# The first 256 tokens' output projection, memory attention and feed-forward as a thread of the attention stage

## The chip, the cores and the metric

The kernel runs on one core of a Trainium2 chip. The metric is the device time of one execution in microseconds (us), as the median of several executions. PE is TensorE (PEld its weight loads), DVE is VectorE, ACT is ScalarE, POOL is GpSimd, SP is SyncE, which here only issues transfers (SPq is its queue).

## The reference, cut to what matters

One layer of a hybrid decoder for 1024 prompt tokens and 8 sample tokens, width 1024, in float32:

```python
h = rmsnorm(x, attn_norm_g)
q, k, v, qi, ki, wi, gq, gk, gv, gz, ga, gb = split(h @ w_in)
o_attn = sparse_attend(q, k, v, top 256 keys by the indexer)     # 8 heads of 64, causal
o_gdn  = gated_delta_chunked(conv(gq, gk, gv), ga, gb)           # 4 heads of 128, recurrent over tokens
x = x + concat([o_attn, o_gdn]) @ w_out                          # 1024 x 1024
x = x + mem_attend(rmsnorm(x), mem_k, mem_v, w_mq, w_mo)         # 4 heads, 256 memory tokens
hf = rmsnorm(x)
x = x + (silu(hf @ w_gate) * (hf @ w_up)) @ w_down               # D_FF = 2816
```

Attention and recurrence are causal: a token's row depends on earlier tokens only, and everything from `w_out` on works on each token alone.

## The kernel before, in words

Each projection is done in three products of rounded parts: a weight arrives by one transfer as `raw`, ACT rounds it to `wh` (L124), POOL subtracts to get `wl` (L125), and for each of eight slices of the contraction PE multiplies `wh` by the high and by the low part of the activations and `wl` by the high part (`proj`, L128 to L139). So one weight of 1024 x 128 costs 24 matmuls for a group of tokens. Activations stand transposed, 128 features on the partitions and tokens along the row, in `AH` and `AL`.

Three stages follow each other in `build` (L1811).

1. **Front**: norm of x, input projections, indexer scores, the top-k searches on DVE, and the preparation of the recurrence (`gdn_prep`, and `gdn_invert` for heads 0 and 1).
2. **Attention stage** (L1853 to L1871): `run` (L69) steps six generators in turn, each at a rate: `stage_attend` (query tiles 7 down to 0, four head pairs each), two threads `gdn_scan` (heads 0, 2 and heads 1, 3, each head through its four quarters of 256 tokens), the sample tokens' gather and attention, their recurrence, and `gdn_invert(1)`, a row by row inversion on POOL that the merges of heads 2 and 3 need. The logits use the PSUM banks `al` (two), transposes use `at` (two).
3. **Tail** (`stage_mem`, `stage_ffn`): all 1032 tokens in the groups `GROUPS2` of 512, 256 and 264. `stage_out` multiplies by `w_out`, `mem_q` and `mem_attend` are the memory attention, `mem_out` multiplies by `w_mo`, and the feed-forward goes in batches of four of its 22 blocks of 128 (`gate_up`, then `down`). `stage_mem_kv` (L1506), which makes the keys and values of the memory, runs beside the first `stage_out`.

The generators only set the program order and a priority number (`cur_priority`, L78). At build time the tile framework replays the program against a model of the engines and from that fixes one order for each engine; on the chip each engine works through its list in that order and waits where an operand is late. Every buffer is a slot of a pool with a fixed number of slots, and transfers that SP issues wait in SP's list for their slot.

```python
self.run([self.stage_attend(qs), 1, 0], [self.scan_pair("a", 0, 2), 0.3, 0], [self.scan_pair("b", 1, 3), 0.3, 0],
         [chain(self.stage_sample_rows(), self.stage_sample_attend()), 0.25, 300],
         [chain(*(self.gdn_sample(h) for h in range(4))), 0.2, 0], [self.gdn_invert(1), 1.0, 300])
```

Of the kernel before, what the change touches and what calls it, by code (L numbers as in the profile page):

```python
# [6 lines left out]
F32 = mybir.dt.float32  # L7
# [13 lines left out]
NS = 8  # L21
# [3 lines left out]
GROUPS2 = ((0, 512), (512, 256), (768, 264))  # L25
# [12 lines left out]

class Kernel:
    def __init__(self, tc, ins, outs):  # L40
        self.tc, self.nc, self.i, self.o = tc, tc.nc, ins, outs
        self.side, self.G = [], GROUPS
        self.set, self.set_users = None, []
# [40 lines left out]

    def drain(self):
# [31 lines left out]
    def raw_w(self, kt, n):  # L117
        return self.wp.tile([128, kt, n], F32, name="raw", tag="raw", bufs=2)

    def split_w(self, raw):  # L120
        shape = list(raw.shape)
        wh = self.wp.tile(shape, FR, name="wh", tag="wh", bufs=2)
        wl = self.wp.tile(shape, FR, name="wl", tag="wl", bufs=2)
# [206 lines left out]
    def stage_topk(self):  # L330
# [29 lines left out]
        def search(data, first, bits):  # L360

            V.memset(P, first + float(1 << (bits - 1)))
            for b in range(bits - 1, -1, -1):
                V.tensor_scalar(nb, P[:, na:], -1.0, 0.5, op0=OP.mult, op1=OP.add)
                for j in range(na, n):
                    nk = (tl[j] + 1) * 128
                    x = self.tk.tile([128, 1024], BF, name="tka", tag="sign")
# [58 lines left out]
    def head_norm(self, p, n, gain, out, sq, tag='mm'):  # L426
# [4 lines left out]
        p2 = self.bank(tag, "pss")  # L431
# [56 lines left out]
    def stack_k(self, g):  # L488
# [5 lines left out]
        for c0 in range(0, T, 256):  # L494
# [5 lines left out]
        self.kh.append(h)  # L500
        self.kl.append(l)

    def stack_q(self, i):
        nc = self.nc
        q = self.up.tile([128, 4, 128], F32, name="qld", tag="qld", bufs=1)
        nc.sync.dma_start(q, self.qscr[i // 3][:, :, 128 * (i % 3):128 * (i % 3) + 128].rearrange("t p q -> p t q"))
        qs = self.up.tile([128, 4, 2, 128], FR, name="qst", tag="qst", bufs=2)
# [12 lines left out]
    def attend_logits(self, i, t, qs, P):  # L520

        nc, V = self.nc, self.nc.vector
        nk, g = (i + 1) * 128, t // 2
        bias = self.score[i] if i >= 2 else self.cbias[:, 128 * (1 - i):256]
        for r in range(2):
            L = self.lg.tile([128, 1024], F32, name="L", tag="L", bufs=self.nL)
            st = self.sm.tile([128, 6], F32, name="ast", tag="ast", bufs=8)
            for c, c0 in enumerate(range(0, nk, 512)):
                n = min(512, nk - c0)
                p = self.bank("al", "plg")  # L530
                self.mm(p[:, :n], qs[:, t, r], self.kh[g][:, c0:c0 + n], True, False)
                self.mm(p[:, :n], qs[:, t, r], self.kl[g][:, c0:c0 + n], False, True)
# [9 lines left out]
    def attend_values(self, i, t, P):  # L542
# [3 lines left out]
        q = slice(i * 128, i * 128 + 128)  # L546
# [31 lines left out]
        self.split(ob, self.AH[:, t, q], self.AL[:, t, q])  # L578
        yield

    def stage_attend(self, qs):

        values = None
        for i in range(7, -1, -1):
            if i < 7:
                qs = self.stack_q(i)
            for t in range(4):
                if i == 7 and t == 1:
                    self.stack_k(1)
                P = []  # L590
# [1334 lines left out]
```

## Time and profile before

| | us |
|---|---|
| three runs | 1827.02, 1820.19, 1819.27 |
| median | 1820.19 |
| the profiled execution's own time | 1817.93 |
| its span, first to last instruction | 1816.2 |
| front / attention stage / tail, by the span's clock | 0 to 528 / 528 to 804 / 804 to 1816 |
| mean granted TensorE clock | 0.963 of full speed |

The span starts with the first instruction of the program. Busy times are unions of an engine's instructions; matmuls are pipelined, so the end of a matmul is modelled and a busy PE need not be a full one. In the chain of waits, a piece such as "PE po x20" is 20 matmuls that follow each other, from the issue of the first to the end of the last.

### The profile page before, as it was taken

How to read it: one execution, taken by the hardware profiler on the slowest of the kernel's cores; microseconds unless marked ns; L12 is line 12 of the kernel's file. 1: busy time of each engine (PE TensorE's matmuls, PEld its weight loads, DVE VectorE, ACT ScalarE, POOL GpSimd, SP SyncE). 2: the span in 40 equal slices, each digit the busy share in tenths (PEclk: the TensorE clock that was granted, in tenths of full speed). 3: DMA queues.
4: the chain of work that ended last, by engine and by line, in shares of the span. 5: the costliest groups of instructions: out<-in, count | busy, mean ns of one | idle time of the engine just before them, and what ended most of it. 6: DMA issues, size and time to landing. Idle time of an engine off the chain costs nothing.

```text
span 1816.2 us, 30619 instructions
## 1 busy us (share of the span) xinstructions
PE 1681.2 (93%) x11316; PEld 1471.5 (81%) x11316; DVE 1042.8 (57%) x2813; ACT 836.4 (46%) x2033; POOL 659.6 (36%) x641
## 2 busy tenths in 40 slices
PE   6998998767869999989998999999999999999998
PEld 5997887656747777767887779999999999999997
DVE  6799997999769877752366355323323323323324
ACT  5667879763446667645566563112112112112112
POOL 1376663445148133225454444222122122122121
PEclk9999998868989999989999999999999999999999
DMA  4133343323342334356222322121121121121013
GB/s 153 50 107 112 112 148 122 105 71 108 123 123 64 80 81 113 100 156 172 83 82 59 93 78 74 46 61 47 33 61 47 31 64 47 30 64 47 30 50 108
DMA packets 229855, 151.42 MB, mean 83 GB/s; under 512 B 29621, under 2 KB 216202, under 8 KB 229698
## 3 DMA queue, kind: packets, MB, share of 16 engines
q1 hardware_dynamic: 210906, 120.38, 22.9%
q0 software_dynamic: 4864, 14.69, 2.8%
q10 hardware_dynamic: 13936, 14.40, 2.3%
q8 instruction: 89, 1.46, 0.3%
q14 instruction: 60, 0.49, 0.1%
HBM read 118.77 MB, written 30.76 MB: 82 GB/s over the span
## 4 chain that ended last, share of the span: by engine, by line
PE 68%; DVE 11%; issue 3%; ACT 2%; DMA 1%; POOL 0%; SPq 0%; ACTq 0%; DVEq 0%; POOLq 0%
PE pu L47 14%; PE pd L47 14%; PE pg L47 14%; PE pm L47 8%; PE po L47 2%; PE pch L47 2%; PE plg L47 2%; PE pt L50 2%; DVE sk_junk L1266 2%; DVE AL L1499 1%; PE halves L47 1%; DVE tkj L349 1%; PE pmq L47 1%; PE pmo L47 1%; PE pmk L47 1%
## 5 line engine op out<-in xcount | busy, mean ns | idle before, releaser
L125 POOL TENSOR_TENSOR wl<-raw,wh 128x1024 fp32r<-128x1024 f32 (+3 forms) x153 | 311.9, 2039 | 745.8 <-ACT wh L124 741.0
L124 ACT CAST wh<-raw 128x1024 fp32r<-128x1024 f32 (+3 forms) x153 | 137.9, 901 | 311.9 <-PE pd L47 200.0
L47 PE MATMUL pm<-AH,wh 128*128 128x384 f32 (+7 forms) x792 | 270.1, 341 | 7.2 <-ACT wh L124 4.0
L47 PE MATMUL pm<-AL,wh 128*128 128x384 f32 (+7 forms) x792 | 263.4, 333 | 0.1
L47 PE MATMUL pm<-AH,wl 128*128 128x384 f32 (+7 forms) x792 | 262.3, 332 | 0.1
L47 PE MATMUL pg<-AL,wh 128*128 128x512 f32 (+2 forms) x528 | 169.7, 322 | 3.2 <-DVE AL L1499 3.1
L47 PE MATMUL pg<-AH,wh 128*128 128x512 f32 (+2 forms) x528 | 169.9, 322 | 1.1 <-DVE a L1753 1.1
L1767 DVE TENSOR_TENSOR xT<-xT,pd 128x512 f32<-128x512 f32 (+2 forms) x144 | 73.1, 512 | 169.5 <-PE pd L47 168.9
L47 PE MATMUL pu<-AL,wh 128*128 128x512 f32 (+2 forms) x528 | 169.5, 321 | 0.0
L47 PE MATMUL pu<-AH,wh 128*128 128x512 f32 (+2 forms) x528 | 169.4, 321 | 0.0
L47 PE MATMUL pu<-AH,wl 128*128 128x512 f32 (+2 forms) x528 | 168.8, 320 | 0.0
L47 PE MATMUL pg<-AH,wl 128*128 128x512 f32 (+2 forms) x528 | 168.8, 322 | 0.0
L47 PEld LDWEIGHTS pm<-AH,wh 128*128 128x128 f32 (+1 forms) x792 | 154.6, 195 | 15.3 <-ACT wh L124 5.4
L47 PEld LDWEIGHTS pm<-AL,wh 128*128 128x128 f32 (+1 forms) x792 | 154.4, 195 | 6.9 <-issue 1.3
L47 PEld LDWEIGHTS pm<-AH,wl 128*128 128x128 f32 (+1 forms) x792 | 153.6, 194 | 5.9 <-issue 1.1
L47 PE MATMUL pd<-ah,wh 128*128 128x512 f32 (+2 forms) x432 | 139.2, 323 | 0.0
L47 PE MATMUL pd<-al,wh 128*128 128x512 f32 (+2 forms) x432 | 138.3, 320 | 0.0
L47 PE MATMUL pd<-ah,wl 128*128 128x512 f32 (+2 forms) x432 | 137.7, 320 | 0.0
L1745 DVE TENSOR_TENSOR sg<-pg,rs 128x256 f32<-128x256 f32 (+2 forms) x66 | 34.0, 515 | 151.0 <-PE pg L47 142.3
L47 PEld LDWEIGHTS pg<-AL,wh 128*128 128x128 f32 x528 | 100.1, 190 | 11.8 <-DVE AL L1499 4.3
L47 PEld LDWEIGHTS pg<-AH,wh 128*128 128x128 f32 x528 | 100.0, 189 | 9.5 <-DVE a L1753 1.4
L1753 DVE TENSOR_TENSOR a<-pu,rs 128x256 f32<-128x256 f32 (+2 forms) x66 | 34.0, 516 | 128.2 <-PE pu L47 128.2
(647 smaller groups left out, 4196.8 us busy)
## 6 DMA issues: line engine op xcount, KB each, us to landing
raw<-in_w_gate SPq DMA_DIRECT2D x26, 512.0 KB
raw<-in_w_up SPq DMA_DIRECT2D x26, 512.0 KB
raw<-in_w_in SPq DMA_DIRECT2D x24, 512.0 KB
raw<-in_w_down SPq DMA_DIRECT2D x40, 256.0 KB
raw<-in_w_out SPq DMA_DIRECT2D x16, 512.0 KB
scrG<-y ACTq DMA_DIRECT2D x32, 192.0 KB
x<-in_x_prompt SPq DMA_DIRECT2D x8, 512.0 KB
xn<-in_x_prompt SPq DMA_DIRECT2D x8, 512.0 KB
```

The source lines that it names most:

```text
L47: return self.nc.tensor.matmul(out, lhsT, rhs, start=start, stop=stop)
L50: return self.nc.tensor.transpose(out, in_, self.ident[:p, :p])
L124: self.nc.scalar.copy(wh, raw)
L125: self.nc.gpsimd.tensor_sub(wl, raw, f32(wh))
L349: V.tensor_scalar(junk()[:, :(i + 1) * 128], data[i], t[:, j:j + 1], None, op0=op, op1=OP.add, accum_out=cnt[:, j:j + 1])
L1266: V.tensor_scalar(junk[:, j % 4, :N], data[:, :N], t, None, op0=op, op1=OP.add, accum_out=cnt[:, j:j + 1])
L1499: nc.vector.scalar_tensor_tensor(self.AL[:, k, s], self.xT[:, k, s], gain[:, k:k + 1], f32(self.AH[:, k, s]), op0=OP.mult, op1=OP.subtract)
L1745: V.tensor_mul(sg[:, :n], p[:, :n], self.rs[:, g0:g0 + n])
L1753: V.tensor_mul(a[:, :n], p[:, :n], self.rs[:, g0:g0 + n])
L1767: V.tensor_add(x, x, p[:, :n])
```

## The change

A class `Part` holds one set of tokens with its own activations, residual, banks and pools. Part A is tokens 0 to 255, part B is tokens 256 to 1023 and the 8 sample tokens, in groups of 512 and 264. Part A's whole tail is the generator `back_a`, stepped beside the attention stage; part B's is `back_b`, after it. Every weight of the tail is therefore loaded and split once for A and again for B. To have part A's inputs early, attention starts with query tiles 1 and 0 of both key groups, each scan starts with quarter 0 of both of its heads, and a first `run` steps these, with `gdn_invert(1)` at rate 8, until `readyA` counts 12 finished pieces. Attention's results of later tokens go to a DRAM scratch `scrM` and are read back and split by `gather_mix` before part B. `stage_mem_kv` moves to the front, ahead of `stage_ab`. The PSUM banks `al` and `at` go from two to one each, and two banks `fa` serve part A. Weights come in halves of four slices (`load_half`), three slots of each kind in the attention stage and four in the tail. `stack_k` keeps one key group at a time.

```diff
-GROUPS2 = ((0, 512), (512, 256), (768, 264))
+TA = 256
+GROUPS_A = ((0, TA),)
+GROUPS_B = ((TA, 512), (768, 264))
...
-        h, l = (self.pp.tile([128, T], FR, name=f"k{x}{g}") for x in "hl")
+        h, l = (self.pp.tile([128, T], FR, name=f"k{x}", tag="k" + x, bufs=1)[:, :n] for x in "hl")
...
-        self.split(ob, self.AH[:, t, q], self.AL[:, t, q])
+        if i < 2:
+            q = slice(i * 128, i * 128 + 128)
+            self.split(ob, self.A.AH[:, t, q], self.A.AL[:, t, q])
+            self.readyA += 1
+        else:
+            nc.sync.dma_start(self.scrM[t, :, 128 * i - TA:128 * i - TA + 128], ob)
...
+        for g, tiles in ((0, (1, 0)), (1, (1, 0)), (1, range(7, 1, -1)), (0, range(7, 1, -1))):
+            if tiles:
+                ks = self.stack_k(g, (tiles[0] + 1) * 128)
+            for i in tiles:
+                qs = self.stack_q(i, g)
+                for t in (2 * g, 2 * g + 1):
...
+        while h // 2 not in self.inverted:
+            yield
...
-        units = [(h, quarter) for h in heads for quarter in range(4)]
+        units = [(h, 0) for h in heads] + [(h, quarter) for h in heads for quarter in range(1, 4)]
...
+    def load_half(self, src, kt, n):
+
+        m = kt // 2
+        a, b = self.load_w(src[:128 * m], m, n), self.load_w(src[128 * m:], m, n)
...
+    def back_a(self):
+
+        A = self.A
+        while self.readyA < 12:
+            yield
+        yield from self.stage_out(A, 0)
+        yield from self.mem_q(A, 0)
+        yield from self.both(A, (0, 0))
+        yield from self.mem_out(A, 0)
+        yield from self.ffn(A, self.fu)
+
+    def gather_mix(self):
+
+        nc, B = self.nc, self.B
+        for k in (4, 5, 6, 7, 0, 1, 2, 3):
+            x = self.unit("xm", [128, T - TA])
+            nc.sync.dma_start(x, self.scrM[k])
+            self.split(x, B.AH[:, k, 0:T - TA], B.AL[:, k, 0:T - TA])
+        self.split(self.smx, B.AH[:, :, T - TA:NT - TA], B.AL[:, :, T - TA:NT - TA])
+
+    def back_b(self):
+
+
+        B = self.B
+        self.gather_mix()
+        self.run([self.stage_out(B, 0), 1.0, 0])
+        self.run([self.stage_out(B, 1), 1.0, 0], [chain(self.mem_q(B, 0), self.both(B, (0, 0), (0, 256))), 0.4, 0])
+        self.run([self.mem_q(B, 1), 1.0, 0], [self.mem_out(B, 0), 1.5, 0])
+        acts = [self.room(B, self.au) for _ in range(4)]
+        gate_up = lambda *g: chain(*(self.gate_up(B, f, a, *g) for f, a in enumerate(acts)))
+        self.run([gate_up(0), 1.5, 0], [self.both(B, (1, 0)), 1.0, 0], [self.mem_sample(B), 6.0, 0])
+        self.run([self.mem_out(B, 1), 1.0, 0])
+        self.run([gate_up(1), 1.0, 0])
...
         self.gains()
+        self.stage_mem_kv()
         self.stage_ab()
...
-        self.nb = {"al": 2, "at": 2, "po": 1, "ga": 1, "gb": 1}
+        self.nb = {"al": 1, "at": 1, "po": 1, "ga": 1, "gb": 1, "fa": 2}
...
+        self.wp = P(name="wA", bufs=1, side="right")
+        self.wb = 3
...
-        self.run([self.stage_attend(qs), 1, 0], [self.scan_pair("a", 0, 2), 0.3, 0], [self.scan_pair("b", 1, 3), 0.3, 0],
+        attend, sa, sb = self.stage_attend(), self.gdn_scan("a", 0, 2), self.gdn_scan("b", 1, 3)
+        first = lambda: self.readyA >= 12
+        self.run([self.until(attend, first), 1.0, 0], [self.until(sa, first), 1.0, 0], [self.until(sb, first), 1.0, 0],
+                 [self.gdn_invert(1), 8.0, 300])
+        self.run([attend, 1, 0], [sa, 0.3, 0], [sb, 0.3, 0],
                  [chain(self.stage_sample_rows(), self.stage_sample_attend()), 0.25, 300],
-                 [chain(*(self.gdn_sample(h) for h in range(4))), 0.2, 0], [self.gdn_invert(1), 1.0, 300])
+                 [chain(*(self.gdn_sample(h) for h in range(4))), 0.2, 0], [self.back_a(), 1.1, -100])
...
+        self.wb = 4
```

## Rows read from the trace of the kernel before

**Rows 1.** The page's first part: busy us of each engine over the span.

```profile
PE 1681.2 (93%) x11316; PEld 1471.5 (81%) x11316; DVE 1042.8 (57%) x2813; ACT 836.4 (46%) x2033; POOL 659.6 (36%) x641
```

**Rows 2.** Busy time of each engine by stretch; the first column is the stretch.

```profile
core 0: us, PE busy (x) PEld busy (x) DVE busy (x) ACT busy (x) POOL busy (x), PEclk, DMA share, GB/s
...
18.00:46.00 28.00, 24.18 (x140) 20.66 (x141) 18.48 (x36) 15.51 (x39) 3.65 (x2) 0.94 0.23 66
...
528.00:590.00 62.00, 56.48 (x506) 41.81 (x507) 55.69 (x184) 38.15 (x103) 46.23 (x69) 0.94 0.31 83
...
528.00:778.00 250.00, 243.32 (x2175) 188.16 (x2176) 196.99 (x801) 167.86 (x544) 99.28 (x132) 0.98 0.34 92
778.00:804.00 26.00, 17.86 (x102) 12.28 (x102) 17.82 (x76) 11.57 (x51) 3.36 (x5) 0.75 0.31 85
804.00:870.00 66.00, 63.61 (x342) 52.33 (x342) 15.50 (x26) 33.27 (x69) 34.74 (x20) 0.97 0.67 194
870.00:1142.00 272.00, 255.93 (x1702) 220.96 (x1701) 143.54 (x239) 150.28 (x317) 126.78 (x85) 0.97 0.26 77
...
1142.00:1780.00 638.00, 638.00 (x4043) 577.58 (x4043) 200.70 (x338) 112.87 (x185) 137.64 (x77) 1.00 0.16 46
```

**Rows 3.** The chain of waits, 700 to 800 us: start, us, what.

```profile
717.43 0.65 PE plg L47 x2
718.08 1.24 PE po L47 x20
719.32 1.88 PE pkqs L47 x16
```

**Rows 4.** PE's groups by shape, 528 to 778 us: busy us, mean ns.

```profile
L47 PE MATMUL po<-pt,v 128*64 128x128 f32 x564 | 50.5, 286 | 0.8 <-ACT pt L567 0.8
L50 PE MATMUL pt<-ident,L 128*128 128x128 f32 x285 | 48.8, 283 | 1.1 <-ACT L L104 0.6 <-ACT pt L567 0.5
L47 PE MATMUL plg<-kh,qst 128*128 128x512 f32 x48 | 24.9, 518 | 13.4 <-DMA vb<-scrV 12.8 <-DVE ast L533 0.4
...
L47 PE MATMUL po<-ident,ast 128*64 128x128 f32 x116 | 11.9, 274 | 0.0
...
L47 PE MATMUL pcm<-sr_rv,sr_hot 128*16 128x32 bf16 x256 | 8.9, 176 | 0.3 <-DVE sr_rv L1361 0.3
```

**Rows 5.** The chain of waits in the tail: start, us, what.

```profile
1108.14 5.77 PE pg L47 x48
...
1142.73 11.35 PE pg L47 x72
```

**Rows 6.** Matmuls of `stage_mem_kv`: ns min, median, max, first and last start.

```profile
L47 PE MATMUL pmk<-mh,wh x32: 276/279/393, 826.5 to 862.8; 128*128 128x256 f32 x32
```

**Rows 7.** POOL in order of time: first and last rows of `gdn_invert(1)`.

```profile
515.43 0.24 POOL L836 TENSOR_TENSOR invT<-invY 64x30 f32<-64x30 f32 x1 [8.01 <-issue]
...
599.17 0.62 POOL L844 COPY invT<-invY 64x256 f32<-64x256 f32 x1 [0.16 <-DMA scrY<-invT]
```

**Rows 8.** Instructions on two tiles, ns and first start: the inversion; the recurrence's outputs.

```profile
L836 POOL TENSOR_TENSOR invT<-invY x60: 230/545/1142, 380.7 to 585.5; 64x30 f32<-64x30 f32 x4, 64x58 f32<-64x58 f32 x4, 64x84 f32<-64x84 f32 x4, 64x108 f32<-64x108 f32 x4
L837 POOL TENSOR_TENSOR invY<-invY,invT x60: 260/575/1776, 381.0 to 585.8; 64x30 f32<-64x30 f32 x4, 64x58 f32<-64x58 f32 x4, 64x84 f32<-64x84 f32 x4, 64x108 f32<-64x108 f32 x4
...
L50 PE MATMUL pot<-ident,o x32: 270/273/475, 613.5 to 797.7; 128*128 128x128 f32 x32
```

**Rows 9.** The page's costliest groups: splitting the weights.

```profile
L125 POOL TENSOR_TENSOR wl<-raw,wh 128x1024 fp32r<-128x1024 f32 (+3 forms) x153 | 311.9, 2039 | 745.8 <-ACT wh L124 741.0
L124 ACT CAST wh<-raw 128x1024 fp32r<-128x1024 f32 (+3 forms) x153 | 137.9, 901 | 311.9 <-PE pd L47 200.0
```

**Rows 10.** All engines' groups, 528 to 778 us: the logits' evacuation.

```profile
L533 DVE CUSTOM_DVE_ANT_0 L<-plg,score 128x512 f32<-128x512 f32 (+1 forms) x80 | 46.8, 590 | 9.6 <-PE plg L47 5.3 <-PE pt L50 2.5 <-PE pks L50 1.0
```

**Rows 11.** SP's waits: us in total, times, longest.

```profile
SPq L114 <- POOL wl L125: 1077.7, 140, 27.3
...
SPq L918 <- PE pch L47: 18.9, 16, 3.3
```

More of the change, by code (lines that the diff above doesn't have):

```diff
@@ L36, in f32, with __init__, cols, act @@
     return ap.bitcast(F32)
+class Part:
+    def __init__(self, groups, AH, AL, xT, rs, sq, banks, bt, big):
+        self.G, self.AH, self.AL, self.xT, self.rs, self.sq = groups, AH, AL, xT, rs, sq
+        self.bank, self.bt, self.big, self.mq = banks, bt, big, {}
+        self.base = groups[0][0]
+    def cols(self, g):
+        g0, n = self.G[g]
+        return slice(g0 - self.base, g0 - self.base + n)
+    def act(self, g):
+        s = self.cols(g)
+        return lambda k: (self.AH[:, k, s], self.AL[:, k, s])
 class Kernel:
@@ L83, in run, with until @@
                             break
+    @staticmethod
+    def until(gen, done):
+        while not done() and next(gen, "end") != "end":
+            yield
     def drain(self):
@@ L423, in stage_topk, with head_norm @@
             yield
-    def head_norm(self, p, n, gain, out, sq, tag='mm'):
+    def head_norm(self, p, n, gain, out, sq, tag='mm', bank=None):
         nc = self.nc
@@ L1509, in stage_mem_kv @@
         nc.sync.dma_start(gb, self.i["mem_norm_g"].to_broadcast([128, D]))
[L1510 removed]
+        mh, ml = ([self.unit("m" + x, [128, 4, 256], FR) for _ in range(2)] for x in "hl")
         for t in range(2):
@@ L1754, in gate_up, with down @@
             V.tensor_mul(a[:, :n], a[:, :n], sgs[g][:, :n])
-            self.split(a[:, :n], *act[g])
+            self.split(a[:, :n], *act(g))
             yield
-    def down(self, f0, acts, last):
+    def down(self, pt, f0, acts, last):
         nc, V = self.nc, self.nc.vector
@@ new lines, in store_y, with room @@
+        if pt is self.B:
+            p = pt.bank("tp", "py")
+            self.tr(p[:NS, :128], pt.xT[:, o, T - pt.base:NT - pt.base], 128)
+            y = pt.bt("y", [NS, 128])
+            nc.scalar.copy(y, p[:NS, :128])
+            nc.scalar.dma_start(self.o["y_sample"].rearrange("b o d -> (b o) d")[:, cs], y)
+    def room(self, pt, pool):
+        n = pt.G[-1][0] + pt.G[-1][1] - pt.base
+        u = pool.tile([128, 2, n], FR, name="a2", tag="a2")
+        return lambda g: (u[:, 0, pt.cols(g)], u[:, 1, pt.cols(g)])
@@ L1799, in stage_ffn, with ffn @@
+    def ffn(self, pt, pool, acts=()):
+        F, C = 22, 4
+        acts, f0 = list(acts), 0
+        groups = range(len(pt.G))
         while f0 < F:
-            n = len(acts)
-            nxt = []
+            while len(acts) < C and f0 + len(acts) < F:
+                acts.append(self.room(pt, pool))
+                yield from self.gate_up(pt, f0 + len(acts) - 1, acts[-1], *groups)
+            n, nxt = len(acts), []
             if f0 + n < F:
-                nxt.append(gate_up(f0 + n))
@@ L1804, in stage_ffn @@
-            self.down(f0, acts, f0 + n >= F)
-            f0 += n
-            while nxt and len(nxt) < C and f0 + len(nxt) < F:
-                nxt.append(gate_up(f0 + len(nxt)))
-            acts = nxt
+                nxt.append(self.room(pt, pool))
+                yield from self.gate_up(pt, f0 + n, nxt[0], *groups)
+            yield from self.down(pt, f0, acts, f0 + n >= F)
+            acts, f0 = nxt, f0 + n
+    def back_a(self):
+        A = self.A
+        while self.readyA < 12:
+            yield
+        yield from self.stage_out(A, 0)
[3 more added lines that the diff above has]
+        yield from self.ffn(A, self.fu)
@@ new lines, in gather_mix @@
+    def gather_mix(self):
[16 more added lines that the diff above has]
+        self.run([gate_up(1), 1.0, 0])
+        self.mkp.release()
+        self.au0, self.au = self.au, self.tc.alloc_tile_pool(name="auC", bufs=6)
+        for _ in self.ffn(B, self.au, acts):
+            pass
```

429 lines of the change are left out of this document (202 added, 227 removed).

## The prediction, made before the change was run

> **What bounds the kernel now.** I read the page's busy times first, then the same by stretch, then the pieces of the chain of waits inside the attention stage, and last the helpers: POOL's inversion, the weight splits, SP's waits. PE is busy 93% of the span [rows 1], so the stages have to be taken one by one. In the tail from 1142 to 1780 us PE is busy all 638 us at full clock [rows 2], and its price there is plain: 72 matmuls of a block take 11.35 us, the 48 of the two smaller groups 5.77 us [rows 5], so a matmul over 256 or 264 tokens costs 0.120 us and one over 512 costs (11.35 - 5.77) / 24 = 0.233 us. Cost goes by tokens; a weight used twice with half the tokens costs PE nothing more. The change can therefore win only where PE now stands idle, and it means to win that in the attention stage.
>
> **How much is idle there** is the question that decides. By the busy row, PE works 243.32 of the 250 us from 528 to 778 [rows 2]: 7 us idle. That view flatters, as matmuls overlap. The weight loads are busy 188.16 of 250 us [rows 2]: 62 us idle. Between these ends I price the 2175 matmuls by the pieces of the chain in which they follow each other [rows 3, 4]: 680 `po` of 20 in 1.24 us, 42 us; 48 pairs of `plg` over 512 keys at 0.65, 31 us; the 48 shorter pairs at half of that, 16 us; 256 `pcm`, 9 us; the other 1047 at 1.88 / 16, 123 us. That is 221 us; with the quarter of a microsecond or so by which each piece's last matmul outlasts its issue taken out, some 205. I take 214, so 36 us are idle. To that comes the edge from 778 to 804 us, with 102 matmuls or some 10 us of issue in 26 us [rows 2], 16 us idle. **52 us is all that there is to win**, and not all of it can be had.
>
> Here a rule of the Trainium skill speaks for the change. "Perfetto Trace Analysis", section "Identifying the Most-Contended Engine", says that matmul busy time is no measure of headroom and weight-load busy time is. By it a quarter of the stage would be free, 62 us in place of my 36; that is the first rival below. The dense tail shows 577.58 us of weight loads in 638 us [rows 2], so that here a full PE reads 91% and not 100%.
>
> **The change, part by part.**
>
> *The moved work.* Part A costs 8 x 24 matmuls for `w_out`, 2 x 24 for `w_mq`, 48 for `w_mo`, 44 x 24 for gate and up, and 22 x 8 x 3 for down: 1872 x 0.120 = 224 us, and some 8 us for its share of the memory attention and the transposes, 232 us. It leaves the tail and comes into the attention stage, so by itself it is worth nothing.
>
> *The wait for part A's inputs.* `back_a` needs quarter 0 of all four heads, and heads 2 and 3 need `gdn_invert(1)`. That ran on POOL from 515 to 600 us among other work [rows 7]. Its 60 row steps have medians of 0.545 and 0.575 us over both inversions [rows 8], so about 34 us for one, and with its end and the four stores some 45 us if it goes first; then a merge, a chain and an output. The recurrence's first output came at 613.5 us before [rows 8], without any wait for an inversion. With all of it stepped first I put the start of part A at 600 us, between 585 and 630. Until then PE has attention alone while both scans wait for the inversion: I take 45 of 72 us issued, between 36 (half) and 57 (as dense as 528 to 590 at best).
>
> *Both together.* From 600 us on PE has 214 + 10 - 45 + 232 = 411 us of issue. Part A's feed-forward, 1584 matmuls or 190 us, can run as densely as in the tail. For the other 221 us I take the density of the stretch 870 to 1142, where several threads share PE too: 288 matmuls over 512 columns at 0.233 and 1414 others at about 0.115 are 230 of 272 us, 85% [rows 2, 5]. So 190 + 221 / 0.85 = 450 us. Ends: all dense, 415; all at 85%, 484. The stage then takes 72 + 450 and an edge of 15 us (drain and `gather_mix`, eight loads through two slots, each rounded and subtracted; the edge before had 16 us idle), between 5 and 25. That is 537 against 276 us, **+261**.
>
> *Helpers.* Part A's weights are loaded and split a second time: 79 weights' worth, 41 MB. POOL gets 79 x 2.04 = 161 us beside its 99, ACT 79 x 0.90 = 71 us beside 168 [rows 2, 9], over 522 us: hidden behind PE. The 41 MB are 90 GB/s over 450 us beside 92 now; 804 to 870 us moved 194 GB/s with PE busy 63.61 of 66 us [rows 2], so they fit. Each SP issue of a weight waits for its slot, as now [rows 11], and now the recurrence's loads stand behind such waits; if this cover goes it is the third rival. `scrM` adds 64 KB stores and the read back, in the edge above. Halved weights cost a second issue and a second fixed part on ACT and POOL, hidden.
>
> *One bank for the logits.* A tile's matmuls (0.65 us) and its evacuation (mean 0.590 us [rows 10]) now follow each other: 96 of them are about 100 us of a 450 us stage, so part A's matmuls fill the gap. Nothing on its own; at worst the 57 us of evacuations.
>
> *Memory keys and values.* 96 matmuls at 0.120 us [rows 5, 6] and some transposes leave the tail, -14 us. In the front PE is busy 24.18 of 28 us already from 18 to 46 us [rows 2], and what follows is longer by what is put ahead: +10, between +4 and +20.
>
> *The rest of the tail.* Its 1012 us lose 232 and 14. Stalls between memory attention and feed-forward stay, since they are chains and not volume, with less of other matmuls to fill them: +5, between -10 and +20. **-241**.
>
> **Sum.** 1816.2 + 10 + 261 - 241 = 1846 us of span. The profiled execution took 1817.93 us, 1.7 over its span, and the median of the runs is 2.3 above that: 1850 us. A measurement of this kernel tells 0.5%, some 9 us, from no change.
>
> **The rivals.**
>
> 1. *The quarter is really free* (faster). If PE needs 188 and not 214 us in the stage, the rest is 196 - 45 + 232 = 383 us. As attention's own gaps then take part A's matmuls, I put it at 95%, 403 us, and the edge at 10: a stage of 485, +209, and 1798 us. For it speaks the weight-load row, against it that `po` and `pkqs` follow each other without a gap in the chain [rows 3]. 0.25.
> 2. *Gains and costs cancel.* Part A starts by 590, PE is 97% dense after: about 1820 us. 0.15.
> 3. *One late transfer stalls all* (slower still). In PE's fixed order part A's matmuls stand behind attention's. The recurrence's loads (`knat`, `vb`, `qkt`) wait already now for slots, 16 times and up to 3.3 us [rows 11]; behind SP's waits for weight slots they come later, and PE stands with part A's ready matmuls behind them. At 78% the 411 us take 527: 1927 us. It decides once the stalls pass 75 us over the 24 recurrence units. 0.11.
> 4. *Part A is not beside but behind.* Its priority number is 100 behind the others and it starts late. If attention drains first, the 52 us stay idle, and the 42 us of part A outside its feed-forward run alone; at the 45 of 72 us of the start they take 67, 25 more. 1816 + 10 + 25 + 5 of the tail and 4 to the median: 1860 us. 0.04.
>
> My forecast, slower by about 30 us, gets 0.45. **Chances**: faster by over 0.5% is rival 1, 0.25; within 0.5% rival 2, 0.15; slower the rest, 0.60. **Range**: the forecast's own, with density (415 to 484 for 450 us), start, edge and front together, is 1815 to 1890; it is stretched to 1796, which takes in half of rival 1, and to 1900, which leaves rival 3 out.
>
> **What would show it.** Windows of the new profile: front longer by 10 us to the first `plg`; the first `w_out` matmuls of part A near 600 us; the attention stage 537 us long, with weight loads busier than 75% but under 91%; a tail of some 771 us with the feed-forward as dense as now. It is wrong if the stage ends in under 490 us (the idle share was larger than priced), if part A starts before 570 us, or if the tail shrinks by much more than 241 us (its stalls went with its volume). Rival 3 would show as PE waits ended by transfers or by SP.

## The result and the profile after

The changed kernel takes 1984.82 us (median of four runs, 1980.73 to 1987.37) against 1820.29 us beside it on the same chip: **a ratio of 1.0893, 95% interval 1.086 to 1.0926**. The profiled execution spans 1979.0 us, 163 more than before. The direction was forecast; the size, 30 us, was not.

The page's first part answers to [rows 1]: PE executes the same 11316 matmuls, in a smaller share of a longer span, and ACT and POOL are busy 157 and 218 us longer.

```profile
PE 1754.2 (89%) x11316; PEld 1521.9 (77%) x11316; DVE 1075.8 (54%) x2786; ACT 993.0 (50%) x2296; POOL 877.2 (44%) x881
```

Three marks cut both spans: the first `plg` (530.4 us before, 579.6 after), the first `w_out` matmul of the tail (803.0 before, 1204.5 for part B after), and the end. The front is 49 us longer, the attention stage with its edge 352 us (624.9 against 272.6), the tail 239 us shorter (774.5 against 1013.2); 49 + 352 - 239 is 162. Busy time of the engines by stretch, as in [rows 2]:

```profile
core 0: us, PE busy (x) PEld busy (x) DVE busy (x) ACT busy (x) POOL busy (x), PEclk, DMA share, GB/s
8.00:51.00 43.00, 18.86 (x88) 16.13 (x89) 28.65 (x46) 26.95 (x65) 4.69 (x2) 0.80 0.46 153
51.00:69.00 18.00, 14.58 (x105) 13.33 (x103) 4.71 (x8) 8.85 (x17) 7.22 (x4) 0.91 0.31 71
580.00:680.00 100.00, 77.22 (x415) 60.68 (x415) 53.83 (x214) 44.16 (x155) 42.62 (x71) 0.63 0.41 110
680.00:1142.00 462.00, 436.20 (x3634) 383.18 (x3632) 272.20 (x765) 299.78 (x703) 251.25 (x222) 0.96 0.41 119
1142.00:1205.00 63.00, 38.65 (x191) 29.66 (x189) 22.73 (x72) 21.87 (x52) 20.61 (x25) 0.62 0.49 143
1205.00:1489.00 284.00, 261.96 (x1468) 212.32 (x1468) 118.57 (x188) 151.95 (x311) 151.69 (x126) 0.95 0.35 105
1489.00:1950.00 461.00, 461.00 (x2613) 403.22 (x2612) 143.36 (x221) 100.09 (x178) 142.12 (x109) 1.00 0.21 61
```

Four places stand out: 43 us of front with 88 matmuls; 100 us at the start of the stage with 415, at a granted clock of 0.63 (most of it at 1.2 GHz); 462 us in which PE looks full but its matmuls, priced as in the prediction (part A's at 0.120 us, the others by [rows 3, 4]), are 398 us of issue, 86%; and an edge of 63 us at 0.62. The tail of B has the dense feed-forward that was expected.

**The front.** SP's issues of the changed kernel from 7 to 62 us: start, us, what.

```profile
7.80 3.42 SPq L137 DMA_DIRECT2D raw<-in_w_mk  x2
...
20.73 3.49 SPq L137 DMA_DIRECT2D raw<-in_w_mv  x2
...
34.50 0.36 SPq L1554 DMA_DIRECT2D gb<-in_mem_norm_g  x1
35.68 4.33 SPq L1559 DMA_DIRECT2D x<-in_mem_prompt  x2
60.48 0.38 SPq L265 DMA_DIRECT2D raw<-in_w_in  x1
```

One of SP's waits there: us in total, times, longest.

```profile
SPq L265 <- POOL wl L148: 20.5, 1, 20.5
```

The memory's weights take both `raw` slots from 8 us on, though they are multiplied only from 51.3 us, when the memory tokens have come in behind all other tokens and been normed. `stage_ab`'s weight waits 20.5 us in SP's list and gets a slot at 60 us, and its first matmul comes at 69.6 us in place of 18.2.

**The start of the stage.** The chain of waits of the changed kernel, 621 to 640 us: start, us, what.

```profile
621.77 1.27 POOL invY L867
...
623.93 2.53 DMA scrY<-invT
...
627.19 1.05 POOL ao L909 x2
628.24 2.07 DMA scrY<-invT
...
631.06 1.95 DMA scrY<-invT
...
633.76 1.93 DMA scrY<-invT
...
635.75 1.80 DMA xu<-scrY
...
637.69 1.04 PE halves L65 x4
```

The row steps of `gdn_invert(1)` end at 621.7 us; four copies with their stores and a load, each transfer some 2 us, later PE may do the merges of heads 2 and 3. They stand first in its list, with attention and part A behind them. The 60 row steps began at 563.1 us and are 30.8 us of work in 58.6 us: POOL has 18 other instructions among them, also the first halves of part A's weights, for which it waits 6.4 us:

```profile
563.13 0.25 POOL L864 TENSOR_TENSOR invT<-invY 64x30 f32<-64x30 f32 x1 [8.35 <-DMA invY<-scrA]
...
589.76 1.27 POOL L148 TENSOR_TENSOR wl<-raw,wh 128x512 fp32r<-128x512 f32 x1 [6.39 <-ACT wh L147]
```

PE in order of time at the same place:

```profile
625.50 0.80 PE L65 MATMUL plg<-kh,qst 128*128 128x512 f32 x1 [0.79 <-DVE ast L555]
626.10 0.63 PE L65 MATMUL plg<-kl,qst 128*128 128x512 f32 x1
627.51 0.80 PE L65 MATMUL plg<-kh,qst 128*128 128x512 f32 x1 [0.79 <-DVE ast L555]
628.11 0.63 PE L65 MATMUL plg<-kl,qst 128*128 128x512 f32 x1
637.69 1.04 PE L65 MATMUL halves<-xu,ao 128*128 128x32 f32 x4 [8.95 <-DMA xu<-scrY]
```

Two faults are seen at once: with one bank each tile of logits starts 2.0 us after the last (at 1.2 GHz here), of which 0.8 is a wait for the evacuation, and then PE stands 9 us. `w_out` of part A has its first 12 matmuls at 601 to 604 us, 18 of 192 before 677, and runs steadily only from 683 us.

### The profile page after: what moved, and what is told of

It reads as the page before. It is cut to its first block, busy times and chain, and to the rows that moved or that the text cites. A ratio compares the mean times of both kernels' runs of the same rounds, so it can differ in the third digit from the quotient of the medians.

```text
span 1979.0 us, 32161 instructions
## 1 busy us (share of the span) xinstructions
PE 1754.2 (89%) x11316; PEld 1521.9 (77%) x11316; DVE 1075.8 (54%) x2786; ACT 993.0 (50%) x2296; POOL 877.2 (44%) x881
## 4 chain that ended last, share of the span: by engine, by line
PE 58%; DVE 13%; DMA 4%; ACT 4%; issue 3%; POOL 2%; SPq 0%; ACTq 0%; POOLq 0%; DVEq 0%
PE pg L65 12%; PE pd L65 12%; PE pu L65 12%; PE pm L65 6%; PE po L65 2%; PE pch L65 2%; DVE sk_junk L1297 2%; PE pt L68 1%; PE plg L65 1%; DVE tkj L372 1%; PE halves L65 1%; PE pmo L65 1%; PE pmq L65 1%; DVE y L757 1%; DVE ALB L1543 1%
## 5 line engine op out<-in xcount | busy, mean ns | idle before, releaser
L148 POOL TENSOR_TENSOR wl<-raw,wh 128x512 fp32r<-128x512 f32 (+2 forms) x389 | 532.6, 1375 | 755.7 <-ACT wh L147 718.2
L147 ACT CAST wh<-raw 128x512 fp32r<-128x512 f32 (+2 forms) x389 | 248.9, 643 | 439.0 <-PE pd L65 154.4
L65 PE MATMUL pd<-a,wh 128*128 128x256 f32 (+2 forms) x1056 | 253.3, 332 | 6.9 <-DVE xTA L1775 2.2
L65 PE MATMUL pm<-AH,wh 128*128 128x384 f32 (+5 forms) x600 | 207.4, 346 | 7.3 <-ACT raw L751 7.1
L65 PEld LDWEIGHTS pd<-a,wh 128*128 128x128 f32 x1056 | 181.6, 196 | 26.6 <-issue 8.8
L65 PE MATMUL pm<-AL,wh 128*128 128x384 f32 (+5 forms) x600 | 200.8, 335 | 0.0
L65 PE MATMUL pm<-AH,wl 128*128 128x384 f32 (+5 forms) x600 | 200.3, 334 | 0.0
L65 PE MATMUL pd<-a,wl 128*128 128x264 f32 (+2 forms) x528 | 174.2, 331 | 4.4 <-POOL wl L148 4.4
L65 PE MATMUL pg<-AHB,wh 128*128 128x512 f32 (+1 forms) x352 | 121.5, 345 | 1.1 <-ACT AHB L1542 1.1
L65 PE MATMUL pg<-AHB,wl 128*128 128x512 f32 (+1 forms) x352 | 120.8, 343 | 0.0
```

The costliest lines, as they stand in the source:

```text
L65: return self.nc.tensor.matmul(out, lhsT, rhs, start=start, stop=stop)
L147: self.nc.scalar.copy(wh, raw)
L148: self.nc.gpsimd.tensor_sub(wl, raw, f32(wh))
```

## The experiments

Each run is beside runs of the kernel before on the same chip (1817.5 to 1821.8 us); ratios are to it. "Stage" is from the first `plg` to part B's first `w_out` matmul.

**What the stage costs without part A.** The feed-forward of part A was left out first, then part A as a whole.

```diff
         yield from self.mem_out(A, 0)
-        yield from self.ffn(A, self.fu)
+        for o in range(KD):
+            self.store_y(A, o)
+            yield
```

> Part A does its output projection and memory attention, but its feed-forward is left out (y of its rows is the residual before it). Its 1584 feed-forward matmuls are 190 us of issue. Theory (the feed-forward is dense and fits well, the stalls are at the start and in the chains): the run is 185 to 200 us shorter than the changed kernel, 1785 to 1800 us. Rival (the feed-forward's weights, halved, split on POOL and mixed into TensorE's fixed order, are what stalls the stage): 215 us or more shorter, 1770 us or less. Filling (the feed-forward takes gaps): under 170 us shorter, 1815 us or more.

Measured 1788.07 us, 0.9829 (0.9791 to 0.9866): 197 us less for 190 us of matmuls. Dense, as theorized; it fills nothing and stalls little on balance.

```diff
-        yield from self.stage_out(A, 0)
...
-        yield from self.ffn(A, self.fu)
+        self.nc.sync.dma_start(self.o["y_prompt"][0, 0:TA], self.i["x_prompt"][0, 0:TA])
+        yield
```

> Part A is left out (its rows of y are only copied from x by one transfer); the early order, the single banks, scrM and part B stay. From the first plg to the first matmul of part B the kernel before took 274 us and the changed kernel 625. Theory (the new order costs by itself and leaves gaps that part A cannot fill, as one late inversion and its round trips stand first in TensorE's order): 320 to 345 us without part A, so that its 232 us of matmuls cost 280 to 305 us where they are now, more than their own price; the run then takes some 1690 us. Rival (the order is nearly free, part A's mixing in is what costs): 276 to 300 us, so that part A costs 325 us or more; some 1650 us.

Measured 1744.36 us, 0.9588 (0.9551 to 0.9625), stage 389.6 us. The new order and banks cost more than either theory had: 117 us over the stage before. All of part A then costs 235 us of stage for 232 us of matmuls. The stage without it had 159 us of idle weight loads (next row, of that run), yet part A came out at its full price.

```profile
579.00:968.00 389.00, 316.79 (x2258) 229.65 (x2258) 222.43 (x856) 188.81 (x582) 100.59 (x144) 0.78 0.29 81
```

**What the 117 us are.** From there, step by step back to the old stage, always without part A: two banks each for logits and transposes; then the old order of the scans; then the old order of the attention's tiles.

```diff
-        self.nb = {"al": 1, "at": 1, "po": 1, "ga": 1, "gb": 1, "fa": 2}
+        self.nb = {"al": 2, "at": 2, "po": 1, "ga": 1, "gb": 1}
```

> Part A left out as in the run without it (1744 us, 390 us from the first plg to part B against 274 before), and the logits and the transposes get their two PSUM banks each back; the early order stays. Theory (the single banks stretch the whole stage: a tile's matmuls and its evacuation follow each other): the stage falls to 310 to 335 us, the run to 1665 to 1690 us. Rival (the early order does it, with the inversion, the merges and the two scans in TensorE's fixed order): the stage stays over 365 us, the run over 1718 us.

Measured 1701.76 us, 0.9341 (0.9314 to 0.9368), stage 341.3 us: the single banks are 43 us. That lies between the two theories; about as much is left for the order.

```diff
-        units = [(h, 0) for h in heads] + [(h, quarter) for h in heads for quarter in range(1, 4)]
+        units = [(h, quarter) for h in heads for quarter in range(4)]
...
-        self.run([self.until(attend, first), 1.0, 0], [self.until(sa, first), 1.0, 0], [self.until(sb, first), 1.0, 0],
-                 [self.gdn_invert(1), 8.0, 300])
...
-                 [chain(*(self.gdn_sample(h) for h in range(4))), 0.2, 0], [self.back_a(), 1.1, -100])
+                 [chain(*(self.gdn_sample(h) for h in range(4))), 0.2, 0], [self.gdn_invert(1), 1.0, 300], [self.back_a(), 1.1, -100])
```

> Part A left out, two banks each, query tiles 1 and 0 first as in the change, but the scans in their old order (each head through its four quarters), without the first run up to readyA and with the inversion at its old rate. Theory (the early quarters of heads 2 and 3, which wait for the inversion and stand in TensorE's order ahead of all else, are the 42 us): within 12 us of the old order's 1660. Rival (the attention's order, with its short tiles first and stack_k made three times, is): within 12 us of the early order's 1702.

Measured 1670.58 us, 0.9194 (0.9167 to 0.922), stage 311.2 us: 31 of the 42 us are the recurrence's order (27 by the ratios, as the two ran on different chips). Its first 100 us beside the same 100 us with the early order, first of the run with the early order and two banks, then of this one:

```profile
581.00:681.00 100.00, 76.81 (x460) 60.93 (x460) 61.14 (x233) 46.93 (x168) 44.23 (x72) 0.69 0.40 107
```

```profile
580.00:680.00 100.00, 92.69 (x801) 71.83 (x801) 83.38 (x316) 60.49 (x192) 45.49 (x73) 0.82 0.31 84
```

With the early order PE gets through 460 matmuls in that time, with the old order of the scans through 801; the granted clock, 0.69 against 0.82, is part of that.

```diff
-        for g, tiles in ((0, (1, 0)), (1, (1, 0)), (1, range(7, 1, -1)), (0, range(7, 1, -1))):
+        for g, tiles in ((1, range(7, -1, -1)), (0, range(7, -1, -1))):
```

> As the run without part A and with two banks each, and the order as before too: query tiles 7 to 0 (now one key group after the other), each head through its four quarters, no first run that steps all until readyA, the inversion at its old rate. What is left of the change in this stage is scrM, the copy of rows and the read back. Theory (single banks): no more than 20 us under the run with two banks and the early order. Rival (the early order): 40 us or more under it. Both: the stage with its edge takes 285 to 310 us against 274 before, as the read back ahead of part B is new; the run 1640 to 1665 us.

(This run has the edit before it too.) Measured 1660.13 us, 0.9112 (0.9086 to 0.9139), stage 296.0 us: 10 us more for the attention's order (15 by the ratios and by the stage). The last 23 us over the stage before are what is left of the change here, with the read back of `scrM`. So the stage adds up: 273 before, 23 read back and rest, 15 attention's order, 30 recurrence's order, 48 single banks, 41 part A without and 194 with its feed-forward, 624.

**Do the banks still matter with part A in them?** Three ways to give back places with part A complete: a second logits bank for one of part A's; that, with part A's products in the two halves of its one bank; and four half places for part A.

```diff
-        self.nb = {"al": 1, "at": 1, "po": 1, "ga": 1, "gb": 1, "fa": 2}
+        self.nb = {"al": 2, "at": 1, "po": 1, "ga": 1, "gb": 1, "fa": 1}
```

> The logits get two PSUM banks again and part A one in place of two. Theory (the single logits bank costs little once part A runs beside): the 31% dense first part from 563 to 650 us gets shorter by 5 to 15 us, but each of part A's some 240 products now waits for the evacuation of the one before, 0.3 to 0.6 us that other threads fill only in part: +20 to +60 us, about 2020 us in all. Rival (the logits bank is the bound of the stage: 96 tiles of matmuls and evacuations one after the other): faster than the changed kernel by 30 us or more, 1955 us or less.

```diff
+        self.nb = {"al": 2, "at": 1, "po": 1, "ga": 1, "gb": 1}
...
-        bank = lambda tag, name: self.bank("fa", name)
+        fa, turn = self.ps.tile([128, 2, 256], F32, name="fa"), cycle((0, 1))
+        wide = ("pml", "pmt", "pmo")
+        bank = lambda tag, name: self.bank("at", name) if name in wide else fa[:, next(turn)]
```

> The changed kernel with part A complete, but its products (256 columns, half a bank) take turns in the two halves of one bank, and its wide tiles share the transposes' bank; so the logits have two banks again and part A keeps two places. Theory (the single logits bank stretches the stage, and part A's matmuls only come in between): 30 to 70 us faster than the changed kernel, 1915 to 1955 us. Rival (part A fills what the single bank leaves, as I had predicted): within 10 us of 1985. Slower by 15 us or more would mean that a bank's two halves cannot be written and read side by side, or that the transposes' bank is now the bound.

```diff
+        self.nb = {"al": 1, "at": 1, "po": 1, "ga": 1, "gb": 1}
...
+        fa = [self.ps.tile([128, 2, 256], F32, name=f"fa{j}") for j in range(2)]
+        turn = cycle((0, 1, 2, 3))
+        place = lambda j: fa[j % 2][:, j // 2]
+        wide = ("pml", "pmt", "pmo")
+        bank = lambda tag, name: self.bank("at", name) if name in wide else place(next(turn))
```

> Part A's products take turns in four halves of its two banks, its wide tiles go to the transposes' bank; the logits keep their one bank. Theory (evacuation: part A's short products of 12 matmuls, 1.44 us, stand in TensorE's order for a free bank while DVE is late with the addition): 10 to 30 us faster, 1955 to 1975 us. Rival (supply or order): within 10 us of 1985. Slower by 10 us or more: the transposes' bank, now shared with the memory attention, is the dearer one.

Measured 2001.05 (1.0982, 1.0932 to 1.1031), 1999.63 (1.0976, 1.0944 to 1.1008) and 2006.38 us (1.103, 1.0998 to 1.1062): 15 to 22 us slower than the changed kernel, all three; the first falls just short of the 20 to 60 us expected of it, the other two missed both the gain of their theory and the 10 us of their rival. Each gives a place to one thread and takes one from another. In the last two the transposes' bank also took the memory attention's wide tiles, so they do not show by themselves whether halves would help.

The traces show where the bank waits went. PE's groups by shape (busy us, mean ns, idle before), first of the changed kernel from 680 to 1142 us, then of the run without part A from 680 to 930 us:

```profile
L65 PE MATMUL pd<-a,wh 128*128 128x256 f32 x320 | 66.7, 302 | 5.9 <-DVE xTA L1775 2.2 <-DVE sg L1752 2.1 <-DVE a L1761 1.5
...
L65 PE MATMUL pd<-a,wl 128*128 128x256 f32 x160 | 48.8, 305 | 4.4 <-POOL wl L148 4.4
...
L68 PE MATMUL pt<-ident,L 128*128 128x128 f32 x244 | 40.9, 285 | 1.1 <-ACT pt L588 1.1
L65 PE MATMUL plg<-kh,qst 128*128 128x512 f32 x41 | 18.4, 448 | 0.3 <-DVE oss L1473 0.3
```

```profile
L68 PE MATMUL pt<-ident,L 128*128 128x128 f32 x248 | 47.9, 311 | 7.3 <-ACT pt L588 3.7 <-ACT L L127 2.8 <-ACT oss L1466 0.3
...
L65 PE MATMUL plg<-kh,qst 128*128 128x512 f32 x40 | 23.2, 579 | 1.3 <-DVE Ls L1437 0.6 <-DVE ast L555 0.4 <-DVE sst L1088 0.2
```

From the records' start times, the mean from one matmul to PE's next is 0.429 us after a `plg` over 512 keys without part A and 0.288 with it, 0.192 and 0.129 us after a `pt`. Part A **does** fill these waits, (0.141 x 82) + (0.063 x 244) = 27 us. Not all of it is the banks: the granted clock was 0.85 in the stretch without part A and 0.96 with it. At the full clock alone the means are 0.344 and 0.272, 0.170 and 0.124 us, which makes 17 us. Against that, from one of part A's own matmuls to PE's next it takes 0.167 us in `pd`, 0.138 in `pg` and 0.128 in `pu`, with 0.120 as their price: 0.047 x 480 + 0.018 x 528 + 0.008 x 528 = 36 us lost again, some 5 of them at the lower clock.

**Who makes part A's matmuls late?** Part of the chain of waits in the changed kernel, 1003 to 1032 us:

```profile
1003.25 1.28 ACT L119
1004.54 0.63 ACT wh L147
...
1006.93 3.02 DMA raw<-in_w_gate
1010.03 0.63 ACT wh L147
1010.73 1.55 POOL wl L148
1012.30 4.02 DMA raw<-in_w_gate
...
1017.12 1.30 POOL wl L148
1018.46 1.21 PE pg L65 x8
...
1022.05 1.31 POOL wl L148
1023.37 3.15 DMA raw<-in_w_gate
1026.62 0.62 ACT wh L147
...
1028.29 1.28 ACT L119
1030.33 1.28 ACT L119
```

Here the chain is not on PE but goes round through a weight's slot: POOL frees it, 256 KB take 3 to 4 us to come, ACT rounds, POOL subtracts for 1.3 us. Such a half weight feeds 12 matmuls of part A, 1.44 us; in the tail before a weight served four times the tokens. In between stand table loads of 1.28 us (ACT L119). Both were tried. First part A's silu out of exp, without a change of tables:

```diff
-            self.silu(sg[:, :n], sg[:, :n])
+            if pt is self.A:
+                e = pt.bt("se")
+                self.exp(e[:, :n], sg[:, :n], scale=-1.0)
+                V.tensor_scalar(e[:, :n], e[:, :n], 1.0, None, op0=OP.add)
+                V.reciprocal(e[:, :n], e[:, :n])
+                V.tensor_mul(sg[:, :n], sg[:, :n], e[:, :n])
+            else:
+                self.silu(sg[:, :n], sg[:, :n])
```

> Part A's silu is made from exp (ACT exp, DVE add, reciprocal and multiply), so that ScalarE never changes its tables in the attention stage; everything else is the changed kernel. Theory (tables): 36 table loads, 46 us, in 580 to 1190 us, each tied behind all exps ahead of it, couple part A to attention; without them the loads fall from 70 to about 36 and the stage from 612 us to 560 or less, the run to 1935 us or less. Rival (the stage is limited by other small waits of a mixed order): the loads go, 66 DVE instructions of some 0.3 us come, the stage stays within 15 us of 612 and the run between 1970 and 2000 us.

Measured 1979.26 us, 1.0862 (1.0783 to 1.0942). The loads fell from 70 to 34, the run by 6 us, which is no more than the scatter of the two kernels' runs; the 46 us of table loads lie beside other work. The theory fell.

Then no low parts in the stage, as a bound. The third product adds `wh` times the high activations a second time, so part A's results are about doubled (not only rounded more coarsely, as its expectation says); the matmuls are the same in number and size.

```diff
+        if self.wb == 3:
+            return wh, wh
         self.nc.gpsimd.tensor_sub(wl, raw, f32(wh))
```

> In the attention stage no low part of a weight is made at all: part A's third product takes wh again (its result is rounded more coarsely), so POOL loses some 210 us of work there and TensorE's matmuls stay the same. Upper bound of all that the supply of part A's weights by POOL costs. Theory (supply): 25 us or more faster, 1960 us or less. Rival (POOL's splits are hidden, as predicted): within 10 us of 1985.

Measured 1951.57 us, 1.0728 (1.0676 to 1.0781): 33 us less. The supply theory holds; these splits were not hidden. In its trace the means are 0.145 us in `pd`, 0.128 in `pg` and 0.125 in `pu`, 17 us of the gain; the rest lies elsewhere, and with POOL's share gone `pd` still stands 0.025 us over its price. Two versions that keep the result move them to DVE, for the down weights alone, and for half of all weights (on top of the two edits below):

```diff
-        self.nc.gpsimd.tensor_sub(wl, raw, f32(wh))
+        (eng or self.nc.gpsimd).tensor_sub(wl, raw, f32(wh))
...
-            wh, wl = self.load_w(self.i["w_down"][0][128 * f0:128 * (f0 + kt), 128 * o:128 * o + 128], kt, 128)
+            wh, wl = self.load_w(self.i["w_down"][0][128 * f0:128 * (f0 + kt), 128 * o:128 * o + 128], kt, 128,
+                                 V if pt is self.A else None)
```

> Part A's down weights get their low part on DVE and not on POOL; all else is the changed kernel. In 680 to 1142 us part A's pd matmuls come 0.167 us apart on the mean where 0.120 is their price, 23 us too much over 480, and POOL needs 1.3 us for each low part of a weight piece that feeds 12 matmuls, 1.44 us. Theory (supply: POOL sets the pace of the down phases): 10 to 30 us faster, 1955 to 1975 us, and pd at 0.14 us or less. Rival (evacuation and order: pd waits for DVE's additions, and more work on DVE makes it worse): within 10 us of 1985 or slower.

```diff
-                                 V if pt is self.A else None)
+                                 V if pt is self.A and o % 2 else None)
...
+        b = self.load_w(src[128 * m:], m, n, self.nc.vector if self.wb == 3 else None)
```

> The version of the three edits (1952 us), with the low parts of part A's weights shared out: second halves of all weights and every other down weight on DVE, the rest on POOL. Without any low part the changed kernel lost 33 us, with all down weights on DVE 8. Theory (supply by one engine at a time): 5 to 20 us faster than 1952. Rival (DVE, which also empties the banks, gives back what POOL gains): 1950 us or slower.

Measured 1976.53 (1.0866, 1.0821 to 1.0911), 8 us less, and 1934.66 us (1.0647, 1.0616 to 1.0678), 18 us under the version that it starts from. The 8 us are no clearer of the scatter than the 6 above and lie within the 10 us of the rival, though `pd` came 0.145 us apart in place of 0.167 (its theory said 0.14 or less). Shared out it is worth more than moved over.

**Priority.** Part A stepped only after the other threads.

```diff
-                 [chain(*(self.gdn_sample(h) for h in range(4))), 0.2, 0], [self.back_a(), 1.1, -100])
+                 [chain(*(self.gdn_sample(h) for h in range(4))), 0.2, 0])
+        self.run([self.back_a(), 1.0, 0])
```

> Part A runs behind the attention stage and not beside it; the early order, the banks and all else stay. This measures what the overlap gives. Theory (there was little idle time to fill, and mixing costs what it fills): the attention stage up to its last output takes about 310 us (276 before, plus one bank and the inversion first), part A alone 270 to 300 us (224 us of matmuls and the chains of its memory attention), together about the 612 us of the changed kernel, so 1970 to 2010 us in all. Rival (the overlap gives much and only other terms failed): 40 us or more slower than the changed kernel, over 2025 us.

Measured 2024.37 us, 1.111 (1.1062 to 1.1157), 40 us slower. It is no clean measure of "no overlap": the framework still put part A's `w_out` at 604 to 746 us beside attention, and only the feed-forward came late.

**The front.** In the changed kernel `stage_mem_kv` goes behind the scores; then the kernel before gets this one part of the change alone (its results wait in DRAM for the tail).

```diff
-        self.stage_mem_kv()
         self.stage_ab()
...
         self.stage_scores()
+        self.stage_mem_kv()
```

> Only the place of stage_mem_kv within the front differs from the changed kernel: it stands behind the indexer scores and not ahead of stage_ab. Theory (order and slots): in the changed kernel its two weights hold both raw slots from 8 and 21 us on and stage_ab's weight comes only at 60 us, so the front is 49 us longer for some 14 us of TensorE work; behind the scores the first pm goes back to about 18 us, the first plg comes 10 to 20 us after the 530 us of before, and the run takes 1950 us (-35). Rival (the work itself): the memory keys and values cost about 49 us wherever they stand in the front, the first plg stays near 580 and the run near 1985.

> The kernel before with one part of the change alone: stage_mem_kv ahead of stage_ab in the front (its results wait in DRAM for the tail). Theory (its place and the two weight slots cost some 45 to 50 us of the front whatever follows, against 14 to 20 us taken out of the tail): first plg at 575 to 580 us in place of 530, the run at 1840 to 1855 us. Rival (the front only looks longer because the rest of the changed front differs, and this part costs 10 us against 14, as predicted): first plg at 540 to 548, the run at 1810 to 1822 us.

Measured 1970.2 us (1.0812, 1.076 to 1.0864), 15 us and not 35 better: `stage_ab` starts at 18.2 us again, but at 89 and 97 us PE waits 5.8 and 4.2 us for the norm of the memory tokens, their products follow to 118 us, and the first `plg` comes 37 us late. So the place ahead of `stage_ab`, with its slots, accounts for 12 of the 49 us; the other 37 stay when no weight of `stage_ab` has to wait. Where they arise is seen from 70 to 130 us, first of the kernel before, then of this run:

```profile
70.00:130.00 60.00, 59.04 (x357) 55.82 (x355) 54.96 (x109) 38.22 (x78) 36.38 (x41) 1.00 0.26 78
```

```profile
70.00:130.00 60.00, 42.42 (x222) 35.04 (x222) 42.65 (x95) 39.64 (x83) 18.10 (x18) 0.86 0.31 88
```

The second run is the clear one: 1870.11 us, **1.028 (1.0228 to 1.0331), 50 us for this part alone**, more than the 1840 to 1855 us of its theory. Its first `plg` comes 55.7 us late (49 in the changed kernel), its tail begins 60.1 us later than before and its last `w_out` matmul 55.7 later: taking the memory's 96 matmuls out of the tail gave back 4 us.

**The edge and the versions.** The read back from slice 0 on, through five slots; and this with `stage_mem_kv` behind the scores and the down weights on DVE.

```diff
-        for k in (4, 5, 6, 7, 0, 1, 2, 3):
-            x = self.unit("xm", [128, T - TA])
+        for k in range(KD):
+            x = self.mkp.tile([128, T - TA], F32, name="xm", tag="xm", bufs=5)
```

> gather_mix reads back slice 0 first, through five slots and not two. Theory (at the edge TensorE stands 20 us for the last of eight loads through two slots): the stop of 20.2 us ahead of part B's first matmul falls to 10 us or less, the run to 1970 to 1978 us. Rival (the loads start late because the memory of the stage before comes free late, and the slots do not matter): the stop stays over 15 us, the run within 5 us of 1985.

> Three edits together: stage_mem_kv behind the scores (15 us alone), the read back from slice 0 through five slots (17 us alone), and the down weights' low part on DVE. They lie in three different stretches, so they should add: 1953 us from the first two alone, with the third 1925 to 1950 us. The kernel before, 1820 us, is not reached by any theory, as the early order (45 us), the front (some 35 us left) and the new edge stay.

Measured 1967.56 us (1.0815, 1.0777 to 1.0853), 17 us less; PE's wait ahead of part B, first changed, then with this edit:

```profile
PE pm L65 <- ACT AHB L165: 20.2, 1, 20.2
```

```profile
PE pm L65 <- ACT AHB L165: 7.9, 1, 7.9
```

The three together gave 1952.26 us (1.0732, 1.0696 to 1.0768), the sum of the two larger, so that the down weights on DVE added nothing that can be told; with the shared low parts 1934.66, the best here and 6.5% behind the kernel before.

## Why the prediction was off

*Right.* The tail lost 239 us for a forecast of 241. Cost goes by tokens: the feed-forward of part A cost 197 us for 190 priced, part A in all 240 for 232. That the tail comes so near is in part luck: the 14 us for the memory's keys and values were 4 where they were measured, so the rest must have given some 235 us and not 227. The first rival, with the weight loads' idle quarter as room, failed; in the stage without part A those loads idle 159 us, and part A still paid its price. The Trainium skill's "Perfetto Trace Analysis", section "Optimization Strategy", says that interleaving stages whose most-contended engine differs may help. That case is not this one, as PE led the busy rows of both stages (243.32 of 250 us and 638 of 638); here what was needed to interleave them cost more than there was to win.

*Wrong: the front, +10 against +49.* The step "PE is busy 24.18 of 28 us already ..., and what follows is longer by what is put ahead" counted matmuls and left out what they wait for: two `raw` slots held from 8 us for weights that cannot be used before 51 (the first run on the front puts their place at 12 us), and memory tokens that come last in SP's list and are normed before PE can use them. The other 37 us stay behind the scores too. And the 14 us taken from the tail were 4: there the memory's products filled waits.

*Wrong: the stage, +261 against +352.* In the terms of the sum the start took 100 us for 72 (579.6 to 680), the mixed part 462 for 450 and the edge 63 for 15: 88 of the 91 us. Worked out in the same way without part A, the forecast's stage is 72 + 179 / 0.85 + 15 = 298 us; the run without part A took 390. So the miss lies in what the stage itself became, and not in part A's price. Three steps carry it, and a fourth may; they were measured in different runs and need not add up.

1. "I put the start of part A at 600 us": the first matmuls do come at 601.3 us, but by that clock part A's `w_out` runs steadily from 634 (683 less the 49 of the front). The term that was mis-sized is the "some 45 us" for the inversion with its end and its four stores: from 563.1 to 635.7 us they took 72.6, with other work of POOL among them. And PE's list had the merges ahead of attention. Without part A the recurrence's early quarters cost 31 us, the attention's early tiles 10.
2. "An edge of 15 us": 63 us with some 20 us of issue, at a clock of 0.62. The order of the read back was 17 of it.
3. "Helpers ... hidden behind PE": averaged over the stage they are, in the stretches of part A's feed-forward not. A half weight costs POOL 1.3 us for 1.44 us of PE. Without POOL's share the kernel is 33 us faster.
4. "One bank for the logits. Nothing on its own": without part A the single banks, of the logits and of the transposes together, cost 43 us. With part A the cover that I named does come, 27 us of their waits or 17 at the same clock; no run shows what the single banks still cost the complete kernel.

The 450 us for the mixed part were 411 us of issue at 91%; 398 us in 462 are 86%, about my worst case of 85% for all of it. One step of the sum is wrong in itself: 205 us takes the quarter of a microsecond out of the 65 pieces of 16 matmuls alone, and out of all 195 pieces 172 us would be left. That would have made more idle and the forecast faster, further from what was measured. The third rival, a late transfer that stalls all, had the mechanism for the start; it priced 78% and 1927 us, and its place was the inversion's result, not the loads of `knat`, `vb` and `qkt`.

*Open.* Whether part A's two banks alone hold up its down products was not isolated, and the 23 us that the stage keeps with the old order and banks were not split between the read back and the rest. What the lower clock costs was not separated from the waits, and what keeps 37 us in the front behind the scores was not tested.

## What to carry to other kernels

Before work is moved beside a stage, run the stage with everything that the move requires (order, banks, slots) but without the work: here that was already 117 us slower, more than twice the 52 us that I had priced as idle. Price helpers by the piece and not by the stage: halving the tokens per weight doubles what ACT, POOL and the slots must do for each microsecond of PE; here each weight of part A served a quarter of the tokens. And a transfer that is issued early for work that is late takes a slot from work that is due.

## What the hardware showed that I had not expected

PE's granted clock was low where PE worked in small pieces, and not only in its long stops. It stood at 1.2 GHz from 569.5 to 593.4 us, where PE had stopped from 565.0 to 574.3, and again from 610.5 to 671.9 us; that second fall came 18 us before the stop of 9 us, while PE ran short tiles with waits of 0.15 to 0.86 us between them. At the edge it fell at 1153.2 us, 31 us before the stop of 20.2 us, and in the 461 us without a stop it was 1.00. From 680 to 1142 us the median step from one `pd` matmul to PE's next is 0.120 us at 2.4 GHz and 0.214 at 1.2. And ACT's 36 table loads, 46 us in the stage and some of them on the chain of waits, gave no more than 6 us when they were taken out.
